# Forty-six products split a second time instead of thirty-six, in a 4096 x 4096 x 4096 product with GELU

## The chip, the cores and the metric

The kernel runs on one NeuronCore of one Trainium2 chip. The metric is the device time of one execution in microseconds, lower being better; "time" below is the median of several runs, and the profiled execution has its own time beside its span.

## The reference

```python
def reference(a, b):            # a, b: 4096 x 4096 float32
    x = np.matmul(a, b)
    return 0.5 * x * (1 + np.tanh(np.sqrt(2 / np.pi) * (x + 0.044715 * x**3)))
```

The output is 4096 x 4096 float32. The kernel loads A and B as 16-bit floats; checks on the sizes of the inputs, made on the way, choose at the end whether the result stands or a slower general path runs (it does not here).

## The kernel before

**Two levels of seven products.** A and B are cut in halves each way, and the four quadrants of the output come from seven products instead of eight (Winograd's form): P1 = A11 B11, P2 = A12 B21, P3 = S4 B22, P4 = A22 T4, P5 = S1 T1, P6 = S2 T2, P7 = S3 T3, with block sums S1 = A21 + A22, S2 = S1 - A11, S3 = A11 - A21, S4 = A12 - S2, and T1 to T4 likewise of B. In the code S1 lies in the cells SA, S3 in ST, and S2 in SB, where S4 later overwrites it.

The output is made in 16 *groups*: four row blocks (512 rows in each half) by four column blocks (512 columns in each half). In a group each of the seven is a product of 512 x 2048 by 2048 x 512, cut in four *quarters* along the middle (512 each).

An **unsplit** product (`quarters`) is 4 quarters x 4 row tiles x 4 matmuls of 128 x 128 by 128 x 512: 64 matmuls (L535). A **split** one (`split`, `stage`, `part_pe`) applies the same scheme once more inside the product: seven parts of 2 row tiles x 8 matmuls of 128 x 128 by 128 x 256, 112 matmuls (L911), the first of each row of P1's part being 512 wide when it also clears the bank. It asks for four sums of A's inner blocks (`inner_sum`, called 5, 6, 3 and 7 by their parts, L841), for sums of B's inner blocks, and for additions inside the PSUM banks (`copy_part` on ACT, L924; `add_part` on DVE, L928). Two products run in turn, stage by stage, one in bank set X and one in Y (`both`, `run`).

**Where B's operands of a split product come from** is its mode in the table GROUPS: `f` fetches seven pieces from HBM that an earlier group stored; `m` fetches the four quarters and makes the pieces on chip with four sums on DVE (`made_split`); `ms` does that and stores the pieces for later (`made_stored`); `um` leaves the product unsplit but makes and stores the pieces; no entry is unsplit. Every such fetch or store moves 512 KB.

**Order of work.** Groups 0 to 6 read B raw and store T1 to T4 as *units* (`raw_group`); those in RAW_CUT split P3 with `made_here` beside the quarters of P4. Groups 7 to 15 (`late_group`) fetch units. While groups 7 and 11 (TURNS) run, the next row block of A is loaded and turned (`turn_quad`); one quadrant of it is turned ahead, in group 10 (EARLY). Each engine's order is written out by a planner (`Plan`): every operation gets a cost from COST, a due time worked back from PE's order, and a place; PE's order is that of the program text. Fetches go out on POOL's queue, stores on SP's (`dma`, L759).

SBUF holds 28 *cells* of 512 KB: 16 for B, 4 each for SB, SA and ST. A split product takes cells for its quarters or pieces of B and for its sums of A; a cell is handed on in order of time, so a fetch into it waits for PE or DVE to have read what was there. Results leave the banks through `add_bank` (DVE, L1124) and `copy_out` (ACT, L1118), then GELU on ACT (L1102, L1112), then the store.

In the code, `combine2` (L841) is every block or inner sum, and `products` (L535) the unsplit matmuls. The groups' numbers are 0-based; group 12 is the first of the last row block.

Of the kernel before, what the change touches and what calls it, by code (L numbers as in the profile page):

```python
# [75 lines left out]
    "POOL": 0.56, "SP": 0.4,  # L76
}

def modes_of(tail=None, **kw):
    got = {name: mode for mode, names in kw.items() for name in names.split()}
    return got if tail is None else {**got, "tail": tail}
# [15 lines left out]
EARLY = {10: 3}  # L100
TURNS = {7: 2, 11: 3}


class Op:
    __slots__ = ("n", "eng", "dur", "fn", "deps", "succ", "key", "left", "ready", "start", "end", "size", "weight")


class Plan:
# [3 lines left out]

    def add(self, eng, dur, fn, r=(), w=(), size=0, batch=None, after=(), slack=18.0, weight=1.0):
        o = Op()
        o.weight = weight
# [24 lines left out]
        return o  # L140
# [37 lines left out]
    def schedule(self):  # L178
# [23 lines left out]
        while n_done < len(self.ops):  # L202
# [31 lines left out]
            o.start = at  # L234
            free[best] = at + o.dur
            n_done += 1
# [55 lines left out]
def half_path(  # L292
# [455 lines left out]
    def dve(cost, fn, r, w, **kw):  # L748
        return plan.add("DVE", COST[cost], fn, r=r, w=w, **kw)

    def act(cost, fn, r, w, **kw):
        return plan.add("ACT", COST[cost], fn, r=r, w=w, **kw)

# [8 lines left out]
    def c(x):  # L762
        return ("c", x)
# [19 lines left out]

    UNIT, PIECE = {}, {}

    def unit(nb, name):
        if (nb, name) not in UNIT:
            t = f"u{nb}{name}"
            UNIT[nb, name] = dram_pool.tile([P, QPH, CELL], F16, name="k_unit", tag=t)
        return UNIT[nb, name]  # L790

    def piece(nb, name, p):
# [55 lines left out]

    def inner_sum(op, x, y):
        t = new_cell()  # L850
        combine2(cell(t).rearrange("p (jj m) -> p jj m", jj=NJ // 2), [c(t)], x, y, op)
        return t
# [35 lines left out]

    def split(s, a_src, b, bits):
        z = Split()  # L890
        z.s, z.a, z.bits, z.sum = s, a_src, bits, {}
        z.b, z.prepare = b
        return z
# [5 lines left out]
    def part_pe(z, p):  # L899
# [19 lines left out]
        if p in z.sum and p != "6":  # L919
            free_cells.append(z.sum.pop(p))  # L920

    def copy_part(dst, src, cost="part"):
        (d, dt), (x, xt) = dst, src
        act(cost, lambda: nc.scalar.copy(out=d, in_=x), [xt] if xt else [], [dt])  # L924
# [5 lines left out]
    def stage(z, k):  # L930
# [8 lines left out]

        if k == 1:  # L940
            z.sum["5"] = inner_sum(1, a_inner(z.a, "21"), a_inner(z.a, "22"))
            z.sum["6"] = inner_sum(-1, as_inner(z.sum["5"]), a_inner(z.a, "11"))
            for r in range(2):
                copy_part(of("12", r), (zeros[:, 0:1].to_broadcast([P, HC]), None), "zero")
            part_pe(z, "5")
            z.j5 = new_small()
            for r in range(2):
                copy_part(j(z.j5, r), of("12", r))
            part_pe(z, "1")
            for r in range(2):  # L950
                copy_part(of("11", r), of("21", r))
        elif k == 2:
            part_pe(z, "2")
            part_pe(z, "6")
            z.sum["3"] = inner_sum(-1, a_inner(z.a, "12"), as_inner(z.sum["6"]))
            free_cells.append(z.sum.pop("6"))
            j2 = new_small()
            for r in range(2):
                copy_part(j(j2, r), of("21", r))
            for r in range(2):  # L960
                add_part(of("12", r), of("12", r), j(j2, r))
            free_small.append(j2)
        elif k == 3:
            z.sum["7"] = inner_sum(-1, a_inner(z.a, "11"), a_inner(z.a, "21"))
# [454 lines left out]

    sets = {"X": 0}  # L1420

    def late_group(gi, modes, turn=None):

# [4 lines left out]
        cut = {name for name in NAMES if modes.get(name, "u") in ("f", "m", "ms")}  # L1428
        tail_v = "P7" in cut or "P3" in cut and modes.get("tail") == "v"
# [6 lines left out]
        if gi in EARLY or turn:  # L1436
            k = new_unit()
            pairs = (k[0], k[2])
        if gi in EARLY:
            turn_quad(EARLY[gi], "11", slots["a"]["21"], pairs)  # L1440
            free_cells.extend(k)
        source = {
            "P1": raw("11"), "P2": raw("12"), "P5": blk(SA), "P6": blk(SB), "P7": blk(s3), "P3": blk(SB), "P4": raw("22")
        }

        def work(name, s, fresh, done=None, bits=False):
# [4 lines left out]
            b = {"f": fetched, "m": made_split, "ms": made_stored}[mode](nb, name)  # L1451
            return stages_of(split(s, source[name], b, bits), done)

# [39 lines left out]

        x4 = {}
        if turn:
            def p4_done(i, s=X):
                x4[i] = copy_out(s, i)

            run(work("P4", X, True, p4_done))
            turn_quad(turn, "22", slots["a"]["22"], pairs)  # L1500
            if gi - 1 not in EARLY:
                turn_quad(turn, "11", slots["a"]["21"], pairs)
            X, Y = Y, X
        both(("P1", X, True, p1_done, "P6" not in cut), ("P2", Y, not alone, p2_done))
        if last:
            final_answer()
        if turn:
            turn_quad(turn, "12", slots["a"]["11"], pairs)
        both(("P6", X, False, p6_done, not tail_v), ("P5", Y, True, p5_done, not tail_v))
        if last:  # L1510
            final_read()
        block(SB, -1, raw("12"), blk(SB))
        if turn:
            turn_quad(turn, "21", slots["a"]["12"], pairs)

# [5 lines left out]
        def c22_v(i):  # L1521
# [7 lines left out]
            else:  # L1529
                y[i] = new_small()  # L1530
                add_bank(v[i], X, i, y[i])
            out_of(gi, i, 1, 1, y[i])

# [5 lines left out]
        def c21(i):  # L1539
# [5 lines left out]
            else:  # L1545
                r0, c0 = place(gi, i, 1, 0)
                for k, (queue, eng) in enumerate((("SP", nc.sync), ("ACT", nc.scalar))):
# [6 lines left out]
                        r=[("f", f)], size=0.35)  # L1554

        def c21_turn(i):
            f = x4[i]
# [7 lines left out]
        if tail_v:  # L1565
            both(("P7", X, True, c22_v, True), ("P3", Y, True, c12))
            if turn:
                for i in range(RT):
                    c21_turn(i)
            else:  # L1570
                run(work("P4", X, False, c21))
            sets["X"] = Y
        else:
# [5 lines left out]
            elif "P3" in cut:  # L1579
                for i in range(RT):  # L1580
                    add_bank(u[i], Y, i)
                run(work("P4", X, False, c21), work("P3", Y, True, c12))
            else:
                run(work("P4", X, False, c21))
                run(work("P3", Y, False, c12))
            sets["X"] = X
        if turn:
# [53 lines left out]
    with tc.manual_schedule():  # L1641
# [18 lines left out]
        for slot in ("11", "12", "21", "22"):  # L1660
            free_cells.extend(slot_cells(slots["b"][slot]))
        for gi, modes in GROUPS.items():
            if gi == LAST:
                final_checks()
            late_group(gi, modes, TURNS.get(gi))
        plan.emit()
# [37 lines left out]
```

## Time and profile before

| | |
|---|---|
| median of 3 runs | 1529.7 us (1527.08 to 1529.83) |
| profiled execution | 1530.25 us, span 1528.7 us |
| PE matmuls in the profile | 8974, busy 1515.7 us |
| of these 512 columns, unsplit (L535) in the two largest groups | 2176 + 2176 |
| DVE, ACT, POOL busy | 1053.6, 653.9, 460.9 us |
| HBM | 320.34 MB read, 144.71 MB written |
| mean granted TensorE clock | 0.999 |

In a row of a group, the line of the kernel, the engine and the operation come first, then what is written and read by name, sizes and count; after the bar the busy time and the mean of one in ns; after the second bar the idle time just before them and what ended it. A row of the order of time has its start, its length, and in brackets the idle time before it. Matmuls are pipelined, so the length of one alone (380 ns) is not its pace.

### The profile page before, as it was taken

The numbers are of one execution on the slowest core, as the hardware profiler recorded it, in microseconds if no ns is written. First come the engines' busy times: TensorE is split into PE (matmuls) and PEld (weight loads), VectorE is DVE, ScalarE is ACT, GpSimd is POOL, SyncE is SP. The second block draws the span as 40 slices with busy tenths as digits, with TensorE's granted clock in tenths as the row PEclk, the third lists the DMA queues.
The fourth block names the chain that finished last, engine by engine and source line by source line (L and its number), as shares of the span: only waits on it lengthen the run. The fifth ranks groups of instructions, "written<-read, shape, count | busy, mean of one in ns | idle before, by whom it ended". The sixth has DMA issues, their size and how long they took to land.

```text
span 1528.7 us, 23988 instructions
## 1 busy us (share of the span) xinstructions
PE 1515.7 (99%) x8974; PEld 878.8 (57%) x8974; DVE 1053.6 (69%) x1236; ACT 653.9 (43%) x1483; POOL 460.9 (30%) x831
## 2 busy tenths in 40 slices
PE   9999999999999999999999999999999999999998
PEld 4444454544445545455446666556456858887684
DVE  2596868847678598794377655664468987977682
ACT  5445244464954545446742221523453323231332
POOL 7765341442205334123411112213220213223130
PEclk9999999999999999999999999999999999999999
DMA  9999599999949999979987878979995667878593
GB/s 175 196 208 220 98 284 322 243 255 303 251 171 229 284 289 279 338 180 265 280 267 273 294 243 279 303 272 281 270 247 196 244 220 249 296 255 306 199 316 136
DMA packets 199467, 382.84 MB, mean 250 GB/s; under 512 B 20144, under 2 KB 110512, under 8 KB 199344
## 3 DMA queue, kind: packets, MB, share of 16 engines
q0 software_dynamic: 140592, 236.51, 65.2%
q1 hardware_dynamic: 58608, 144.60, 24.9%
q8 instruction: 72, 1.18, 0.3%
q14 instruction: 51, 0.42, 0.1%
q10 hardware_dynamic: 144, 0.13, 0.0%
HBM read 320.34 MB, written 144.71 MB: 304 GB/s over the span
## 4 chain that ended last, share of the span: by engine, by line
PE 89%; DMA 6%; DVE 2%; POOL 1%; issue 1%; ACT 1%; ACTq 0%; POOLq 0%; DVEq 0%
PE acc L535 59%; PE acc L911 27%; PE acc L570 2%; DMA stage<-in_a_dram 2%; DMA bR<-in_a_dram 2%; DMA bR<-in_b_dram 2%; DMA bR<-k_unit 1%; POOL stage L437 1%; DVE y L549 1%; DVE aD L520 1%; POOL bR L437 0%; DVE aT L412 0%; ACT y L1158 0%; DVE aD L549 0%; POOL bR L759 0%
## 5 line engine op out<-in xcount | busy, mean ns | idle before, releaser
L535 PE MATMUL acc<-bR,aT 128*128 128x512 f16 x2176 | 478.7, 380 | 2.4 <-DMA bR<-k_unit 2.4
L535 PE MATMUL acc<-bR,aD 128*128 128x512 f16 x2176 | 478.4, 379 | 0.8 <-ACT y L1112 0.8
L535 PEld LDWEIGHTS <-aD 128*128 128x128 f16 x2272 | 222.4, 98 | 264.6 <-issue 4.9
L535 PEld LDWEIGHTS <-aT 128*128 128x128 f16 x2240 | 219.6, 98 | 261.7 <-issue 4.9
L759 POOL DMA_DIRECT2D bR<-k_unit x255 | 145.6, 573 | 560.5 <-PE acc L535 270.3
L841 DVE TENSOR_TENSOR bR<-bR 128x2048 f16<-128x2048 f16 x181 | 218.0, 1221 | 84.7 <-DMA bR<-in_b_dram 38.1
L911 PE MATMUL acc<-bR 128*128 128x256 f16 x1984 | 232.4, 273 | 0.0
L759 POOL DMA_DIRECT2D bR<-in_b_dram x288 | 155.4, 544 | 250.2 <-PE acc L535 154.0
L911 PEld LDWEIGHTS <-bR 128*128 128x128 f16 x1984 | 194.1, 98 | 30.6 <-DVE bR L841 0.3
L1124 DVE TENSOR_TENSOR y<-acc,y 128x512 f32<-128x512 f32 x240 | 154.9, 686 | 41.7 <-PE acc L911 23.0
L1192 ACT ACTIVATE y<-bR 128x1024 bf16<-128x1024 f16 x128 | 129.6, 1051 | 108.4 <-DVE y L1197 91.0
L924 ACT COPY y<-acc 128x256 f32<-128x256 f32 x144 | 53.5, 371 | 205.3 <-PE acc L911 205.2
L1102 ACT ACTIVATE y<-y 128x512 f32<-128x512 f32 x180 | 107.6, 627 | 70.6 <-DVE y L1124 69.5
L1118 ACT COPY y<-acc 128x512 f32<-128x512 f32 x116 | 66.5, 585 | 157.2 <-PE acc L535 108.9
L911 PE MATMUL acc<-bR,aD 128*128 128x256 f16 (+1 forms) x864 | 103.8, 274 | 0.0
L928 DVE TENSOR_TENSOR acc<-acc,y 128x256 f32<-128x256 f32 x144 | 59.7, 429 | 59.7 <-ACT y L924 37.1
L1158 ACT ACTIVATE y<-bR 128x512 f16<-128x512 f16 x128 | 80.5, 629 | 38.1 <-DMA bR<-in_a_dram 29.2
L841 DVE TENSOR_TENSOR aD<-aT,aD 128x2048 f16<-128x2048 f16 x60 | 72.9, 1220 | 32.3 <-PE acc L535 32.3
L841 DVE TENSOR_TENSOR aD<-aD,aT 128x2048 f16<-128x2048 f16 x60 | 72.5, 1220 | 29.0 <-PE acc L535 29.0
L911 PEld LDWEIGHTS <-aD 128*128 128x128 f16 x864 | 84.5, 98 | 13.0
L1197 DVE TENSOR_TENSOR y<-y 128x1024 bf16<-128x1024 bf16 x120 | 82.6, 688 | 13.2 <-ACT y L1192 9.6
L412 DVE STREAM_TRANSPOSE aT<-stage 128x1024 uint32<-128x1024 uint32 (+1 forms) x27 | 35.7, 1349 | 63.3 <-DMA stage<-in_a_dram 53.8
(86 smaller groups left out, 1273.8 us busy)
## 6 DMA issues: line engine op xcount, KB each, us to landing
bR<-k_unit POOLq DMA_DIRECT2D x255, 512.0 KB, 6.8
out_dram<-y SPq DMA_DIRECT2D x251, 256.0 KB, 6.5
k_unit<-bR SPq DMA_DIRECT2D x112, 512.0 KB, 6.5
bR<-in_b_dram POOLq DMA_DIRECT2D x384, 128.0 KB, 6.7
k_piece<-bR SPq DMA_DIRECT2D x36, 512.0 KB, 5.5
bR<-k_piece POOLq DMA_DIRECT2D x36, 512.0 KB, 5.8
bR<-in_a_dram POOLq DMA_DIRECT2D x64, 256.0 KB, 8.4
stage<-in_a_dram POOLq DMA_DIRECT2D x48, 256.0 KB, 7.7
```

The source lines that it names most:

```text
L535: nc.tensor.matmul(acc, sa[:, j // 2, i * P : (i + 1) * P, j % 2], sb[:, j, :], start=start and j == 0, stop=stop and j == 3, skip_group_c ...
L759: return plan.add(queue, COST[queue], lambda: eng.dma_start(out=dst, in_=src), r=r, w=w, size=MOVE[what], weight=weight, **kw)
L841: nc.vector.tensor_tensor(out=dst, in0=xa, in1=ya, op=ALU.add if op > 0 else ALU.subtract)
L911: nc.tensor.matmul(PS[s][i][:, :] if wide else PS[s][i][:, w * HC : (w + 1) * HC], sa[:, j // 2, r * P : (r + 1) * P, j % 2], rhs(j, wide) ...
L924: act(cost, lambda: nc.scalar.copy(out=d, in_=x), [xt] if xt else [], [dt])
L928: dve("part", lambda: nc.vector.tensor_tensor(out=d, in0=xa, in1=ya, op=ALU.add), [xt, yt], [dt])
L1102: act("gelu", lambda: nc.scalar.activation(t, t, ACT.Gelu_apprx_tanh), [("f", f)], [("f", f)])
L1118: act("copy", lambda: nc.scalar.copy(out=sm(f), in_=bank(s, i)), [], [("f", f), ("p", s, i)])
L1124: dve("add", lambda: nc.vector.tensor_tensor(out=sm(g), in0=bank(s, i), in1=sm(f), op=ALU.add), [("f", f)], [("f", g), ("p", s, i)])
L1158: act("weigh", lambda x=x, r=r, s=s, f=f: nc.scalar.activation(small[f].bitcast(F16)[:, : 2 * RUN], s[:, x, :], ACT.Square, accum_out=t[:, ...
L1192: act("square", lambda t=t, src=src: nc.scalar.activation(t, src, ACT.Square), [c(cx)], [("f", f)], slack=60.0)
L1197: dve("add16", lambda t=t, u=u: nc.vector.tensor_tensor(out=u, in0=u, in1=t, op=ALU.add), [("f", f)], [("f", e)], slack=60.0)
```

## The change

- Which products are split changes throughout: raw groups 1 and 2 split nothing (RAW_CUT), groups 7 to 15 split 43 products instead of 31, mostly in mode `m`; raw groups 5 and 6 store pieces of P7, and of P6 and P3.
- S1, S2, S3 are made once in a row block and kept; S4 is written into A21's cells, which no product reads after S1 and S3 exist. Groups that turn A keep the old way.
- In groups 8, 9, 13 and 14 P4 is split too. There P3 no longer shares its bank set's content with P4, and in groups 8 and 13 P4 is left over and run at the start of the next group beside P1 (`pending`), which then takes an order of its own.
- Inside a split product sum 6 overwrites sum 5's cell and sum 3 overwrites sum 6's (IN_PLACE). A's inner sums of P1 and P3 are stored in group 12, those of P3 fetched in group 14 (`a_sum`).
- The early turn of group 10 moves from the group's start to its end.
- The planner keeps an engine for EVERY's shorter time per operation (start to start), while the result still counts as ready after COST's time.

```diff
+EVERY = {
+    "sum": 1.145, "sum/2": 0.62, "add": 0.61, "add16": 0.62, "copy": 0.49, "gelu": 0.54, "square": 0.97, "weigh": 0.65,
+    "part": 0.345, "turn": 1.2,
+}
...
-RAW_MAKES = {}
-RAW_CUT = (1, 2, 4, 5, 6)
+IN_PLACE = 3
+RAW_MAKES = {5: ("P7",), 6: ("P6", "P3")}
+RAW_CUT = (4, 5, 6)
 GROUPS = {
-    7: {},
-    8: modes_of(ms="P2 P5 P7"),
-    9: modes_of(ms="P2 P5 P7"),
-    10: modes_of(ms="P2 P5 P7"),
-    11: modes_of(m="P5"),
-    12: modes_of(m="P2 P5 P7 P1 P6"),
-    13: modes_of(f="P2 P5 P7", m="P1 P6 P3"),
-    14: modes_of(f="P2 P5 P7", m="P1 P6"),
-    15: modes_of(f="P2 P5 P7", m="P1 P6"),
+    7: modes_of(m="P1 P6", tail="v"),
+    8: modes_of(m="P4 P5 P6", ms="P7", um="P1", tail="v"),
+    9: modes_of(m="P2 P3 P4 P7", ms="P1 P6"),
+    10: modes_of(m="P1 P2 P5 P6 P7", tail="v", early="end"),
+    11: modes_of(m="P2 P5"),
+    12: modes_of(f="P3 P6", m="P1 P2 P7", store="P1 P3"),
+    13: modes_of(f="P7", m="P1 P2 P5 P6", ms="P3 P4", tail="v"),
+    14: modes_of(f="P6", m="P1 P2 P3 P4 P5 P7", fetch="P3", tail="v"),
+    15: modes_of(f="P7", m="P2 P3 P5 P6"),
 }
-EARLY = {10: 3}
 TURNS = {7: 2, 11: 3}
...
             o.start = at
-            free[best] = at + o.dur
+            free[best] = at + o.every
...
+    def a_sum(z, p, op, x, y, t=None):
+        if z.kept is None:
+            return inner_sum(op, x, y, t)
+        how, *key = z.kept
+        if how == "fetch":
+            t = new_cell() if t is None else t
+            dma("POOL", cell(t), a_piece(*key, p)[:, :], [("as", *key, p)], [c(t)], "unit")
+            return t
+        t = inner_sum(op, x, y, t)
+        dma("SP", a_piece(*key, p)[:, :], cell(t), [c(t)], [("as", *key, p)], "unit")
+        return t
...
+            x5 = z.sum["5"]
             part_pe(z, "5")
+            if IN_PLACE & 1:
+                free_cells.remove(x5)
+                z.sum["6"] = a_sum(z, "6", -1, as_inner(x5), a_inner(z.a, "11"), x5)
...
-            z.sum["3"] = inner_sum(-1, a_inner(z.a, "12"), as_inner(z.sum["6"]))
-            free_cells.append(z.sum.pop("6"))
+            x6 = z.sum.pop("6")
+            z.sum["3"] = a_sum(z, "3", -1, a_inner(z.a, "12"), as_inner(x6), x6 if IN_PLACE & 2 else None)
...
-        block(SB, -1, blk(SA), raw("11"))
+        if new_mb or not held_sums:
+            block(SB, -1, blk(SA), raw("11"))
...
+        if s4_in_slot:
+            if new_mb:
+                s4 = raw("21")
+                for q in range(QPH):
+                    dst, toks = a_quarter(s4, q)
+                    combine2(dst, toks, a_quarter(raw("12"), q), a_quarter(blk(SB), q), -1)
+            held_sums.append(gi)
...
+        if pending:
+            run(pending(), work("P1", X, True, p1_done_f, "P6" not in cut))
...
+            both(("P2", Y, True, p2_done_f), ("P6", X, False, p6_done_f))
...
+            both(("P5", Y, True, p5_done_f), ("P7", X, True, lambda i: c22_v(i), "P4" not in cut))
+            both(("P3", Y, True, lambda i: c12(i), not last), ("P4", X, "P4" in cut, lambda i: c21(i), not last))
+            if modes.get("early") == "end":
+                early()
...
+            elif "P4" in cut:
+                sets["X"] = Y
+                return lambda: work("P4", X, True, c21, True)
```

More of the change, by code (lines that the diff above doesn't have):

```diff
@@ L77, with modes_of @@
 }
-def modes_of(tail=None, **kw):
-    got = {name: mode for mode, names in kw.items() for name in names.split()}
-    return got if tail is None else {**got, "tail": tail}
-RAW_MAKES = {}
-RAW_CUT = (1, 2, 4, 5, 6)
-GROUPS = {
-    7: {},
-    8: modes_of(ms="P2 P5 P7"),
-    9: modes_of(ms="P2 P5 P7"),
-    10: modes_of(ms="P2 P5 P7"),
-    11: modes_of(m="P5"),
-    12: modes_of(m="P2 P5 P7 P1 P6"),
-    13: modes_of(f="P2 P5 P7", m="P1 P6 P3"),
-    14: modes_of(f="P2 P5 P7", m="P1 P6"),
-    15: modes_of(f="P2 P5 P7", m="P1 P6"),
+EVERY = {
+    "sum": 1.145, "sum/2": 0.62, "add": 0.61, "add16": 0.62, "copy": 0.49, "gelu": 0.54, "square": 0.97, "weigh": 0.65,
+    "part": 0.345, "turn": 1.2,
+}
+def modes_of(tail=None, early=None, store="", fetch="", **kw):
+    got = {name: mode for mode, names in kw.items() for name in names.split()}
+    got["kept"] = {**{n: "store" for n in store.split()}, **{n: "fetch" for n in fetch.split()}}
+    return {**got, **{k: v for k, v in (("tail", tail), ("early", early)) if v}}
+IN_PLACE = 3
+RAW_MAKES = {5: ("P7",), 6: ("P6", "P3")}
+RAW_CUT = (4, 5, 6)
+GROUPS = {
+    7: modes_of(m="P1 P6", tail="v"),
[7 more added lines that the diff above has]
+    15: modes_of(f="P7", m="P2 P3 P5 P6"),
 }
-EARLY = {10: 3}
 TURNS = {7: 2, 11: 3}
 class Op:
-    __slots__ = ("n", "eng", "dur", "fn", "deps", "succ", "key", "left", "ready", "start", "end", "size", "weight")
+    __slots__ = ("n", "eng", "dur", "fn", "deps", "succ", "key", "left", "ready", "start", "end", "size", "weight", "every")
 class Plan:
@@ L111, in __init__, with add @@
         self.ops, self.state, self.now = [], {}, BUSY["PE"]
-    def add(self, eng, dur, fn, r=(), w=(), size=0, batch=None, after=(), slack=18.0, weight=1.0):
+    def add(self, eng, dur, fn, r=(), w=(), size=0, batch=None, after=(), slack=18.0, weight=1.0, every=None):
         o = Op()
+        o.every = dur if every is None else every
         o.weight = weight
@@ L748, in dve @@
     def dve(cost, fn, r, w, **kw):
-        return plan.add("DVE", COST[cost], fn, r=r, w=w, **kw)
+        return plan.add("DVE", COST[cost], fn, r=r, w=w, every=EVERY.get(cost), **kw)
     def act(cost, fn, r, w, **kw):
-        return plan.add("ACT", COST[cost], fn, r=r, w=w, **kw)
+        return plan.add("ACT", COST[cost], fn, r=r, w=w, every=EVERY.get(cost), **kw)
     def dma(queue, dst, src, r, w, what, **kw):
@@ L790, in unit, with a_piece @@
         return UNIT[nb, name]
+    def a_piece(mb, name, p):
+        if (mb, name, p) not in A_PIECE:
+            t = f"a{mb}{name}{p}"
+            A_PIECE[mb, name, p] = dram_pool.tile([P, CELL], F16, name="k_asum", tag=t)
+        return A_PIECE[mb, name, p]
     def piece(nb, name, p):
@@ L887, in half_path, with split @@
         pass
-    def split(s, a_src, b, bits):
+    def split(s, a_src, b, bits, kept=None):
         z = Split()
-        z.s, z.a, z.bits, z.sum = s, a_src, bits, {}
+        z.s, z.a, z.bits, z.sum, z.kept = s, a_src, bits, {}, kept
         z.b, z.prepare = b
@@ L963, in stage @@
         elif k == 3:
[L964 removed]
+            z.sum["7"] = a_sum(z, "7", -1, a_inner(z.a, "11"), a_inner(z.a, "21"))
             part_pe(z, "7")
@@ L1418, in raw_group, with late_group @@
             slots["a"] = {"11": old["21"], "12": old["11"], "21": old["12"], "22": old["22"]}
-    sets = {"X": 0}
-    def late_group(gi, modes, turn=None):
+    sets, held_sums = {"X": 0}, []
+    def late_group(gi, modes, turn=None, pending=None):
         mb, nb = groups[gi]
@@ L1435, in late_group, with early, fourth @@
             block(ST, -1, raw("11"), raw("21"))
-        if gi in EARLY or turn:
+        def early():
+            k = new_unit()
+            turn_quad(groups[gi][0] + 1, "11", slots["a"]["21"], (k[0], k[2]))
+            free_cells.extend(k)
+        held_sums.clear()
+        s4_in_slot = not turn and modes.get("early") != "start"
+        if modes.get("early") == "start":
+            early()
[6 more added lines that the diff above has]
+            held_sums.append(gi)
+        if turn:
             k = new_unit()
             pairs = (k[0], k[2])
-        if gi in EARLY:
-            turn_quad(EARLY[gi], "11", slots["a"]["21"], pairs)
-            free_cells.extend(k)
+        def fourth():
+            if not s4_in_slot:
+                block(SB, -1, raw("12"), blk(SB))
         source = {
-            "P1": raw("11"), "P2": raw("12"), "P5": blk(SA), "P6": blk(SB), "P7": blk(s3), "P3": blk(SB), "P4": raw("22")
+            "P1": raw("11"), "P2": raw("12"), "P5": blk(SA), "P6": blk(SB), "P7": blk(s3), "P3": raw("21") if s4_in_slot else blk(SB), "P4": raw("22")
         }
@@ L1451, in work @@
             b = {"f": fetched, "m": made_split, "ms": made_stored}[mode](nb, name)
-            return stages_of(split(s, source[name], b, bits), done)
+            how = modes.get("kept", {}).get(name)
+            return stages_of(split(s, source[name], b, bits, how and (how, mb, name)), done)
         p1, u, v, y = {}, {}, {}, {}
@@ L1492, in both, with p2_done_f, p6_done_f, p1_done_f @@
                 run(work(*xs), work(*ys))
[L1494 to L1514, printed above, removed]
+        def p2_done_f(i):
+            f = new_small()
+            add_bank(p1[i], Y, i, f)
+            out_of(gi, i, 0, 0, f)
+        def p6_done_f(i):
+            if "P6" in cut:
+                u[i] = add_bank(p1[i], X, i)
+            else:
+                free_small.append(p1[i])
+                u[i] = copy_out(X, i)
+        def p1_done_f(i):
+            p1[i] = copy_out(X, i)
+        def p5_done_f(i):
+            v[i] = new_small()
+            add_bank(u[i], Y, i, v[i])
         def c12(i):
@@ L1554, in c21, with p4_done @@
                         r=[("f", f)], size=0.35)
+        if pending:
+            run(pending(), work("P1", X, True, p1_done_f, "P6" not in cut))
+            if last:
+                final_answer()
+            both(("P2", Y, True, p2_done_f), ("P6", X, False, p6_done_f))
+            if last:
+                final_read()
+            fourth()
+            both(("P5", Y, True, p5_done_f), ("P7", X, True, lambda i: c22_v(i), "P4" not in cut))
+            both(("P3", Y, True, lambda i: c12(i), not last), ("P4", X, "P4" in cut, lambda i: c21(i), not last))
+            if modes.get("early") == "end":
+                early()
+            sets["X"] = Y
+            return None
+        x4 = {}
+        if turn:
+            def p4_done(i, s=X):
+                x4[i] = copy_out(s, i)
+            run(work("P4", X, True, p4_done))
+            turn_quad(turn, "22", slots["a"]["22"], pairs)
+            if "early" not in GROUPS.get(gi - 1, ()):
+                turn_quad(turn, "11", slots["a"]["21"], pairs)
+            X, Y = Y, X
+        both(("P1", X, True, p1_done, "P6" not in cut), ("P2", Y, not alone, p2_done))
+        if last:
+            final_answer()
+        if turn:
+            turn_quad(turn, "12", slots["a"]["11"], pairs)
+        both(("P6", X, False, p6_done, not tail_v), ("P5", Y, True, p5_done, not tail_v))
+        if last:
+            final_read()
+        fourth()
+        if turn:
+            turn_quad(turn, "21", slots["a"]["12"], pairs)
         def c21_turn(i):
@@ L1566, in late_group @@
             both(("P7", X, True, c22_v, True), ("P3", Y, True, c12))
+            if modes.get("early") == "end":
+                early()
             if turn:
@@ L1582, in late_group @@
                 run(work("P4", X, False, c21), work("P3", Y, True, c12))
+                if modes.get("early") == "end":
+                    early()
             else:
@@ L1585, in late_group @@
                 run(work("P3", Y, False, c12))
+                if modes.get("early") == "end":
+                    early()
             sets["X"] = X
```

21 lines of the change are left out of this document (14 added, 7 removed).

## The prediction

> **What bounds the kernel now.** I read the page's busy times first, then who PE waited for, then PE's own order of time, then DVE and the DMA landings in the stretches that the change fills.
>
> ```profile
> PE 1515.7 (99%) x8974; PEld 878.8 (57%) x8974; DVE 1053.6 (69%) x1236; ACT 653.9 (43%) x1483; POOL 460.9 (30%) x831
> PE acc L535 <- DMA bR<-k_unit: 2.4, 1, 2.4
> PE acc L535 <- DVE aD L520: 1.8, 1, 1.8
> PE acc L544 <- DVE table L717: 1.5, 1, 1.5
> PE acc L535 <- DVE y L549: 1.0, 2, 0.9
> ```
>
> PE works 99% of the span. The list of its waits (microseconds in total, times, longest) says the same from the other side: four of them pass 1 us, three of those belong to the first group and the start, and only one, 2.4 us for a fetched unit, lies in the groups that the change touches. So the time is the columns that PE streams, plus that one wait. A busy PE could still be a slow one, so I take its pace from starts, not from the modelled durations:
>
> ```profile
> 1059.79 55.42 PE L535 MATMUL acc<-bR,aT 128*128 128x512 f16 x256
> 1115.05 3.62 PE L535 MATMUL acc<-bR,aD 128*128 128x512 f16 x16
> ...
> 1270.33 7.15 PE L911 MATMUL acc<-bR 128*128 128x256 f16 x64
> 1277.32 1.91 PE L911 MATMUL acc<-bR,aT 128*128 128x256 f16 x16
> ```
>
> From 1059.79 to 1115.05 there are 256 matmuls of 512 columns: 0.2159 us each. From 1270.33 to 1277.32 there are 64 of 256 columns: 0.1092 us each, just over half. An unsplit product is 64 of the first, 13.81 us; a split one is 112 of the second, 12.23 us.
>
> **The one wait, and its real price.**
>
> ```profile
> 994.57 1.91 PE L911 MATMUL acc<-bR 128*128 128x256 f16 x16
> 998.87 5.30 PE L535 MATMUL acc<-bR,aT 128*128 128x512 f16 x16 [2.39 <-DMA bR<-k_unit]
> 1004.00 1.25 PE L911 MATMUL acc<-bR 128*128 128x256 f16 x10
> ...
> 998.90:1004.00 5.10, 5.10 (x16) 1.96 (x16) 3.58 (x3) 1.76 (x3) 0.00 (x0) 0.67 0.40 162
> ...
> 112.20 2.82 PE L535 MATMUL acc<-aD 128*128 128x512 f16 x12 [0.85 <-DVE y L549]
> 115.20 1.02 PE L535 MATMUL acc<-aD 128*128 128x512 f16 x4 [0.18 <-DVE y L549]
> 118.08 1.24 PE L535 MATMUL acc<-aD 128*128 128x512 f16 x5 [1.85 <-DVE aD L520]
> ```
>
> The 16 matmuls after the 2.39 us gap last from 998.87 to 1004.00, 5.13 us where 16 x 0.2159 = 3.45 are due: the granted clock in that row of the stretches is 0.67. The wait therefore cost 2.39 + 1.68 = 4.1 us. A gap of 1.85 us at 118.08 has no such tail (1.24 us for 5). So a stall costs its own length up to about 2 us, and 1.7 more from about 2.4. [...]
>
> **The change, part by part.** Counts come from the order of the two built programs.
>
> *PE.* 640 matmuls of 512 columns go (ten products, 64 each) and 1120 split ones come; of the split ones six more than before have 512 columns (the first matmul of P1's part where the bank is cleared). Net: 634 x 0.2159 = 136.9 us out, 1114 x 0.1092 = 121.6 us in: **-15.2 us**. All of it lies on the path, since PE has no other slack. Raw groups 1 and 2 lose their split product, which is in these counts.
>
> *The old wait.*
>
> ```profile
> 954.64 24.22 DMA bR<-in_a_dram x2
> 985.55 13.27 DMA bR<-k_unit
> ```
>
> These two pieces of the chain that ended last come just before it. In group 10 the early turn of the next block's A stood at the group's start, so eight 256 KB loads ran on POOL's queue ahead of the fetches for P1 and P2, and a unit then took 13.27 us. The turn now stands at the end of the group, beside P3 and unsplit P4, where DVE and PE want no new fetch at once. I take the 4.1 us as gone; if another fetch is late there it stays. Bounds: 0 to **-4.1**.
>
> *DVE.* Kept block sums remove 44 sums (S2 and S4 in the second to fourth group of a block, eight each but four in group 11). A split product adds four sums of A and four additions inside the banks; an operand made on chip adds four sums of B. Net over the program: 51 more sums and 8 half ones, 40 more bank parts, 28 more whole-bank additions.
>
> ```profile
> L841 DVE TENSOR_TENSOR bR<-bR 128x2048 f16<-128x2048 f16 x181 | 218.0, 1221 | 84.7 <-DMA bR<-in_b_dram 38.1 <-PE acc L911 16.1 <-DMA bR<-k_unit 13.9
> L1124 DVE TENSOR_TENSOR y<-acc,y 128x512 f32<-128x512 f32 x240 | 154.9, 686 | 41.7 <-PE acc L911 23.0 <-PE acc L535 15.9 <-ACT y L1118 1.4
> L928 DVE TENSOR_TENSOR acc<-acc,y 128x256 f32<-128x256 f32 x144 | 59.7, 429 | 59.7 <-ACT y L924 37.1 <-PE acc L911 21.3
> ...
> 1209.51 1.09 DVE L928 TENSOR_TENSOR acc<-acc,y 128x256 f32<-128x256 f32 x3 [0.44 <-PE acc L911]
> ...
> 1212.90 1.22 DVE L841 TENSOR_TENSOR bR<-bR 128x2048 f16<-128x2048 f16 x1
> 1214.03 1.22 DVE L841 TENSOR_TENSOR bR<-stage 128x2048 f16<-128x2048 f16 x1
> 1215.17 1.88 DVE L1124 TENSOR_TENSOR y<-acc,y 128x512 f32<-128x512 f32 x3
> ...
> 1218.10 2.48 DVE L1124 TENSOR_TENSOR y<-acc,y 128x512 f32<-128x512 f32 x4
> ```
>
> In full durations (1.22, 0.686, 0.429; half sum half of it) that is 51 x 1.22 + 8 x 0.61 + 40 x 0.429 + 28 x 0.686 = 104 us, so DVE 1158 us of some 1512, 77%: never the bound as a whole. What counts is where it sits. Back to back, a sum takes 1.14 us from start to start (1212.90 to 1214.03), a whole-bank addition (2.48 - 0.69)/3 = 0.60, a part (1.09 - 0.43)/2 = 0.33. Now the densest stretches, with A22's products put where they run:
> - Groups 13 and 14 (13 split products and one P4 that slides from 13 into 14, nothing unsplit): PE 196 half-row steps of 8 x 0.1092 = 0.874, with eight wide starts, 172.1 us. DVE 100 sums, 56 parts, 56 additions: 114 + 18.5 + 33.6 = 166.1 us, 97% of PE.
> - Groups 8 and 9: PE 64 x 0.863 + 140 x 0.874 + 0.9 = 178.5; DVE 96 sums, 8 half sums, 40 parts, 52 additions: 109.4 + 4.6 + 13.2 + 31.2 = 158.4, 89%.
> - Groups 5 and 6 gain 4 and 8 sums for P7, P3 and P6's stored pieces, 4.6 and 9.1 us, in groups of 95 us (96 x 0.863 + 14 x 0.874); they had unsplit products to hide in.
>
> ```profile
> 1193.60:1218.00 24.40, 24.40 (x224) 21.88 (x225) 23.79 (x30) 6.97 (x18) 4.73 (x9) 1.00 0.54 186
> 1331.70:1345.50 13.80, 13.80 (x67) 6.23 (x65) 13.54 (x16) 2.91 (x6) 2.36 (x3) 1.00 0.84 321
> ```
>
> In these rows (length, then busy PE, PEld, DVE, ACT, POOL, clock, DMA) DVE is busy 23.79 of 24.40 us and 13.54 of 13.80 while PE never stops: 97% can be held, but shown for 25 us, not for 172. Every small wait of DVE for a bank (0.44 us in the row above) has no spare place in groups 13 and 14. Bounds: 0, if the order fills all of them; 172 x 3% = 5 us, if DVE loses another 3% beyond the 97. I take 2.
>
> *A's sums in place.* P6's sum now overwrites P5's cell, and P3's overwrites P6's. That puts a wait on DVE: the sum for part 6 may start only when PE has read part 5. Behind it in DVE's fixed order stand the next product's sums and the bank parts; PE's part 6 waits for it. Between part 5 and part 6 PE has eight half-row steps (or four and an unsplit quarter, 3.5 us either way), 7.0 us, for one sum of 1.22: covered. Where A's sums are fetched instead of made (P3 of group 14 alone), the same hand-over goes through POOL: behind that fetch stand the 16 unit fetches of group 15.
>
> ```profile
> bR<-k_unit POOLq DMA_DIRECT2D x255, 512.0 KB, 6.8
> ...
> bR<-k_unit POOLq DMA_DIRECT2D x50, 512.0 KB, 8.3
> ...
> bR<-k_piece POOLq DMA_DIRECT2D x12, 512.0 KB, 5.5
> ```
>
> The columns end with median microseconds to landing: over the whole run, in the stretch 900 to 1060 us, and for pieces in group 14 of this kernel. From part 6 read to part 3 needed PE has eight steps, 7.0 us. A 512 KB fetch lands in 5.5 to 8.3: between 0 and 1.5 us late, 0.5 taken.
>
> *DMA.* POOL's fetches of 512 KB go from 291 to 283, SP's stores from 148 to 156: nothing in sum. Group 12 rises from 28 to 42 of them (eight are A's kept sums), with 16 outputs of 256 KB: 26.2 MB in the group's 89 us (32 x 0.863 + 70 x 0.874), 294 GB/s. Groups 8 to 10 of before have 40 and as many outputs, 25.2 MB in 92 us, 274 GB/s, and had one late fetch in three groups. Bounds 0 to 4.1; I take 1.5.
>
> *ACT.* 40 copies out, 20 zero fills and 20 bank copies, under 0.4 us each, on an engine at 43%: hidden; without that cover each is 0.4 us.
>
> **Sum.** The profiled execution took 1530.25 us (span 1528.7). 1530.25 - 15.2 - 4.1 = 1510.9, the floor; + 2 + 0.5 + 1.5 = 1514.9. The three runs have their median 0.55 lower, at 1529.7; I give 1515.
>
> **Rivals.**
> - *DVE becomes the bound* in groups 13 and 14. If the back-to-back overlap is lost because most operations wait singly for PE or ACT, DVE needs 100 x 1.22 + 56 x 0.429 + 56 x 0.686 = 184.4 us against PE's 172.1: 12.3 more, 1510.9 + 12.3 = 1523. For it: single waits of 0.44 us are common where parts are added. Against: overlap holds in the rows above, in a stretch of split products only. [...]
> - *Fetches land late* at the hand-over from one made pair to the next: the next pair's four B quarters may be fetched only into cells that the present pair frees after its parts 7 and 4. One late fetch of 2.4 us costs 4.1. It decides from the fifth: 1510.9 + 5 x 4.1 = 1531, slower than before. With about 18 hand-overs in groups 9 to 15, every second one late gives 1510.9 + 9 x 4.1 = 1548. For it: 8.3 us landings. Against: group 12 of before had the same pattern, four made products in a row, without one wait of PE.
> - *The smaller matmuls don't keep their pace* once nothing else lies between, because the weight load is what sets 0.109. PEld is busy 21.88 of 24.40 us in such a stretch, so it is not. If it were 3% slower, 1114 x 0.1092 x 3% = 3.6 us: 1518.5.
>
> **How the numbers follow.** Forecast, with its sums from 1510.5 to 1518: 0.68. DVE as the bound, up to 1524: 0.14. One to four late fetches, 1518 to 1527: 0.10. Five or more: 0.06. Slow small matmuls: 0.02. The range from 1509.5 (0.5 below the floor with its 0.55, rounded) to 1525 leaves out the last fetch cases. A difference under 0.2%, 3 us, cannot be told from none; so faster is below 1526.6 (0.90), the same 0.04, slower 0.06.
>
> **What would show it.** Right: PE's busy time near 1500, no row of its waits above 2 us in groups 7 to 15, the granted clock 1.00 in every stretch, DVE 95% or more in groups 13 and 14. Wrong: a wait of L923 (split matmuls) for DVE sums adding to 10 us (first rival), for DMA into bR several times with clock below 0.8 after it (second), or a start-to-start pace of split matmuls above 0.111.

## Result and the profile after

The changed kernel takes 1512.45 us (1510.38 to 1512.8) where the kernel before takes 1529.76: the ratio of the two is 0.9877 (95% interval 0.9843 to 0.9911). In a later job on another chip (run e10, the changed kernel once more) it was 1512.67 beside 1528.3, ratio 0.9904 (0.9888 to 0.9920). So it is faster by 1.0 to 1.2%, 16 to 17 us by the medians; 1515 was forecast. The profiled execution took 1512.8 us, its span 1511.2.

The page's busy times and its landings, changed kernel:

```profile
PE 1499.0 (99%) x9454; PEld 924.7 (61%) x9454; DVE 1148.4 (76%) x1372; ACT 672.7 (45%) x1555; POOL 451.9 (30%) x823
bR<-k_unit POOLq DMA_DIRECT2D x259, 512.0 KB, 7.8
```

PE issues 480 matmuls more and is busy 16.7 us less. DVE has gained 95 us and PE is still at 99%. Whom PE waited for, all its rows (microseconds in total, times, longest):

```profile
PE acc L541 <- DVE aD L526: 1.9, 1, 1.9
PE acc L550 <- DVE table L723: 1.5, 1, 1.5
PE acc L541 <- DVE y L555: 1.2, 2, 1.1
PE acc L541 <- ACT y L559: 1.0, 2, 0.6
PE acc L576 <- ACT y L559: 0.7, 1, 0.7
PE acc L923 <- DVE bR L853: 0.5, 2, 0.3
PE acc L923 <- DMA bR<-k_asum: 0.3, 1, 0.3
PE acc L923 <- DVE y L1155: 0.2, 1, 0.2
```

The first five belong to the start and to the first group. Only the last three lie in work that the change touches, 1.0 us in all, and the 2.4 us for a fetched unit is gone; in e10's profile the waits in groups 7 to 15 are down to one of 0.27 us. PE in order of time shows where the last three lines fall, all but 0.16 us of them in group 14:

```profile
678.79 2.12 PE L923 MATMUL acc<-bR,aD 128*128 128x512 f16 x16 [0.16 <-DVE bR L853]
1321.39 2.04 PE L923 MATMUL acc<-bR 128*128 128x256 f16 x16 [0.32 <-DVE bR L853]
1397.21 3.87 PE L923 MATMUL acc<-bR,aT 128*128 128x512 f16 x32 [0.21 <-DVE y L1155]
1401.34 1.92 PE L923 MATMUL acc<-bR 128*128 128x256 f16 x16 [0.26 <-DMA bR<-k_asum]
```

The stretches (columns as in the prediction) from the start of group 13 to the end of group 14, whole and two of its pieces:

```profile
1243.80:1417.20 173.40, 172.60 (x1569) 153.15 (x1568) 161.32 (x207) 61.35 (x152) 38.18 (x69) 1.00 0.76 263
1268.00:1293.00 25.00, 25.00 (x232) 22.40 (x230) 24.99 (x33) 7.63 (x20) 5.42 (x9) 1.00 0.63 205
1363.00:1388.00 25.00, 25.00 (x232) 22.40 (x230) 25.00 (x31) 8.11 (x21) 4.73 (x9) 1.00 0.62 209
```

In 173.4 us PE stops for 0.8. DVE is busy 93% over the whole and without a gap in the two pieces of 25 us; it keeps up, just. The pace of the split matmuls is that of the kernel before: 64 of them take 6.99 us from start to start here, 0.1092 us each.

```profile
1255.85 7.15 PE L923 MATMUL acc<-bR 128*128 128x256 f16 x64
1262.84 1.91 PE L923 MATMUL acc<-bR,aT 128*128 128x256 f16 x16
```

### The profile page after: what moved, and what is told of

It is laid out like the page before. It is cut to its first block, busy times and chain, and to the rows that moved or that the text cites. A ratio compares the mean times of both kernels' runs of the same rounds, so it can differ in the third digit from the quotient of the medians.

```text
span 1511.2 us, 25214 instructions
## 1 busy us (share of the span) xinstructions
PE 1499.0 (99%) x9454; PEld 924.7 (61%) x9454; DVE 1148.4 (76%) x1372; ACT 672.7 (45%) x1555; POOL 451.9 (30%) x823
## 5 line engine op out<-in xcount | busy, mean ns | idle before, releaser
L541 PE MATMUL acc<-bR,aT 128*128 128x512 f16 x1920 | 421.6, 379 | 0.0
L541 PE MATMUL acc<-bR,aD 128*128 128x512 f16 x1792 | 391.5, 379 | 0.0
L853 DVE TENSOR_TENSOR bR<-bR 128x2048 f16<-128x2048 f16 (+1 forms) x251 | 297.6, 1202 | 99.1 <-DMA bR<-k_unit 29.4
L541 PEld LDWEIGHTS <-aT 128*128 128x128 f16 x1984 | 194.0, 98 | 227.1
L541 PEld LDWEIGHTS <-aD 128*128 128x128 f16 x1888 | 184.5, 98 | 224.9 <-issue 4.6
L923 PE MATMUL acc<-bR 128*128 128x256 f16 x2752 | 320.4, 273 | 0.6 <-DVE bR L853 0.3
L923 PEld LDWEIGHTS <-bR 128*128 128x128 f16 x2752 | 269.0, 98 | 38.6 <-DVE bR L853 0.6
L948 ACT COPY y<-acc 128x256 f32<-128x256 f32 x184 | 68.2, 371 | 181.6 <-PE acc L923 174.8
L923 PE MATMUL acc<-bR,aT 128*128 128x256 f16 x1056 | 126.2, 274 | 0.2 <-DVE y L1155 0.2
L923 PEld LDWEIGHTS <-aT 128*128 128x128 f16 x1056 | 103.3, 98 | 14.3 <-issue 0.4
L853 DVE TENSOR_TENSOR aD<-aT 128x2048 f16<-128x2048 f16 x60 | 71.9, 1219 | 46.0 <-PE acc L541 45.3
L923 PEld LDWEIGHTS <-aD 128*128 128x128 f16 x816 | 79.8, 98 | 11.9 <-issue 0.4
```

Source lines behind the costliest of these rows:

```text
L541: nc.tensor.matmul(acc, sa[:, j // 2, i * P : (i + 1) * P, j % 2], sb[:, j, :], start=start and j == 0, stop=stop and j == 3, skip_group_c ...
L853: nc.vector.tensor_tensor(out=dst, in0=xa, in1=ya, op=ALU.add if op > 0 else ALU.subtract)
L923: nc.tensor.matmul(PS[s][i][:, :] if wide else PS[s][i][:, w * HC : (w + 1) * HC], sa[:, j // 2, r * P : (r + 1) * P, j % 2], rhs(j, wide) ...
```

## Experiments

Each is one edit of the changed kernel, or of the kernel before where it says so. Times are medians beside the kernel before on the same chip, whose medians were 1528.66 (e1 to e4), 1529.06 (e5 to e8) and 1528.3 (e9 to e12).

**e1: the early turn's place alone, in the kernel before.**

```diff
-        if gi in EARLY:
-            turn_quad(EARLY[gi], "11", slots["a"]["21"], pairs)
...
             both(("P7", X, True, c22_v, True), ("P3", Y, True, c12))
+            if gi in EARLY:
+                k = new_unit()
+                turn_quad(EARLY[gi], "11", slots["a"]["21"], (k[0], k[2]))
...
```

> The kernel before with one edit: group 10's early turn of the next block's A stands after P7 and P3 instead of at the group's start. Theory (the turn's eight loads held up the fetches of P1 and P2, and that one wait of 2.39 us cost 4.1 with the slow clock behind it): the wait of PE for a fetched unit is gone, clock 1.00 throughout, 1529.7 - 4.1 = 1525.6 us. Rival (the stores of pieces in groups 8 to 10 load the queues, the turn's place is indifferent): the wait stays, 1529 to 1530.

1527.55 us, ratio 1.0003 (0.9985 to 1.0022). In its profile the wait for a fetched unit is gone, so the mechanism holds; the 4.1 us do not show. The two medians differ by 1.1 us, and the interval includes no difference at all.

**e9: the kernel before once more.**

> The kernel before, unchanged, profiled once more. Theory A (the late fetch in group 10 belongs to the kernel): PE waits for a fetched unit near 999 us again, about 2.4 us with a slow clock behind it. Theory B (it was that execution's luck, DMA landings vary): no such wait, span 1525 to 1526.

PE in order of time:

```profile
998.15 3.61 PE L535 MATMUL acc<-bR,aT 128*128 128x512 f16 x16 [1.35 <-DMA bR<-k_unit]
```

The wait is there again, at the same place, but 1.35 us long, and the 16 matmuls behind it take 3.61 us instead of 5.30, at a granted clock of 1.00 from 990 to 1000 us: no slow clock. It belongs to the kernel; its price was one execution's.

**e2: the block sums not kept.**

```diff
-        s4_in_slot = not turn and modes.get("early") != "start"
+        s4_in_slot = False
```

> The changed kernel, with S2 and S4 made anew in every group, in SB: 44 more sums on DVE, nothing else changed. In groups 13 and 14 DVE's work rises by 16 sums to 166.1 + 18.2 = 184.3 us against PE's 172.1. Theory A (DVE stands just under PE there, so the kept sums are what lets the splitting pay): 5 to 12 us of PE waiting for DVE in groups 12 to 15, up to 3 in group 9; 1518 to 1526. Theory B (DVE has room, the kept sums are worth nothing): 1512 to 1514.

1533.44 us, ratio 1.0034 (1.0018 to 1.0050): all of the gain is gone and some more. Its waits of PE for DVE, apart from those of the first group:

```profile
PE acc L923 <- DVE acc L952: 7.7, 4, 3.0
PE acc L923 <- DVE bR L853: 6.9, 8, 1.7
PE acc L923 <- DVE y L1155: 1.7, 1, 1.7
PE acc L541 <- DVE y L1155: 0.8, 1, 0.8
```

They sum to 17.1 us, 0.16 of it before group 7. Each of the 14 stops costs some 0.16 us more than its row says: the wait is counted from the end of the matmul before (0.273 us long), where in an unbroken run the next would have started 0.109 after its start. Before the two longest waits, which end at 1345.83 and 1400.18, DVE did not stop (length, then busy PE, PEld, DVE, ACT, POOL, clock, DMA):

```profile
1340.00:1345.80 5.80, 3.14 (x29) 2.67 (x28) 5.80 (x7) 0.00 (x0) 1.98 (x4) 1.00 0.82 252
1394.00:1400.10 6.10, 3.17 (x30) 2.69 (x28) 6.10 (x9) 0.00 (x0) 1.57 (x3) 1.00 0.88 273
```

So PE waits because DVE has too much to do: theory A, and more than its 12 us of waits, since DVE is late not only in groups 13 and 14 but, by the times of the waits, in 10, 11 and 15 too. With 46 products split, 44 sums of 1.14 us decide between 16 to 17 us gained and 5 lost.

**e3: A22's product left whole in the four groups.**

```diff
-    8: modes_of(m="P4 P5 P6", ms="P7", um="P1", tail="v"),
+    8: modes_of(m="P5 P6", ms="P7", um="P1", tail="v"),
```

and P4 likewise out of groups 9, 13 and 14.

> The changed kernel with P4 unsplit in groups 8, 9, 13 and 14 (42 products split), so nothing slides into the next group. Theory (columns decide): four times 13.81 - 12.23 = 1.58 us more, less 0.9 for eight wide starts that go: 5.5 more, 1518. Rival (the last four cost DVE what they save PE): 1512 to 1514, with fewer waits for DVE.

1518.97 us, ratio 0.9937 (0.9921 to 0.9954), 6.3 to 6.5 us above the changed kernel's medians, which are from other chips. Columns decide: 5.5 were worked out, and no wait of the late groups passes 0.8 us.

**e6: the planner's old view of DVE's and ACT's occupation.**

```diff
-EVERY = {
-    "sum": 1.145, "sum/2": 0.62, "add": 0.61, "add16": 0.62, "copy": 0.49, "gelu": 0.54, "square": 0.97, "weigh": 0.65,
-    "part": 0.345, "turn": 1.2,
-}
+EVERY = {}
```

> The changed kernel, where the planner again takes COST's time for an engine's occupation as well (EVERY empty); the same work, another order on DVE and ACT. Theory A (the order only has to be near right, DVE does what comes): 1512 to 1514. Theory B (with DVE at 97% of PE in groups 13 and 14, an order planned on 1.19 a sum instead of 1.145 makes PE wait in the wrong places): 2 to 6 us of waits of PE for DVE more, 1514 to 1519.

1518.78 us, ratio 0.9932 (0.9917 to 0.9948), 6 us above the changed kernel with the same operations on every engine. Its waits of PE in the late groups:

```profile
PE acc L920 <- DVE bR L850: 2.3, 2, 1.7
PE acc L920 <- ACT acc L945: 1.4, 3, 0.6
PE acc L920 <- DVE acc L949: 1.4, 2, 1.0
```

5.1 us, 3.7 of it for DVE, where the changed kernel has 1.0. So an order planned on the longer times brings some 4 us of waits; the rest of the 6 is not shown to come from the order. In the profiled execution (1519.17 us) 1.7 us were lost elsewhere, in the first group, behind a wait that the changed kernel has as well; the first row of each pair is e6, the second the changed kernel:

```profile
119.61 5.30 PE L538 MATMUL acc<-aD 128*128 128x512 f16 x16 [1.85 <-DVE aD L523]
120.03 3.61 PE L541 MATMUL acc<-aD 128*128 128x512 f16 x16 [1.85 <-DVE aD L526]
...
119.60:124.90 5.30, 5.29 (x17) 2.09 (x17) 2.64 (x4) 1.98 (x4) 4.23 (x8) 0.68 1.14 247
120.03:123.48 3.45, 3.45 (x17) 1.56 (x17) 2.59 (x4) 1.89 (x3) 3.00 (x6) 1.00 1.12 258
```

The same 16 matmuls behind the same wait of 1.85 us ran at a granted clock of 0.68 here and of 1.00 there. All fourteen profiles have this wait; in thirteen the matmuls behind it kept their pace of 0.216 us, only in e6 were they slow.

**e7: A's inner sums neither stored nor fetched.**

```diff
-    12: modes_of(f="P3 P6", m="P1 P2 P7", store="P1 P3"),
+    12: modes_of(f="P3 P6", m="P1 P2 P7"),
...
-    14: modes_of(f="P6", m="P1 P2 P3 P4 P5 P7", fetch="P3", tail="v"),
+    14: modes_of(f="P6", m="P1 P2 P3 P4 P5 P7", tail="v"),
```

> The changed kernel without stored sums of A: group 12 stores none, and P3 of group 14 makes its four on DVE, 4.6 us more of DVE where it is at 97%, for 12 transfers of 512 KB less. Theory A (DVE is full there): 1 to 4 us more of waits for DVE, 1513 to 1517; the 0.3 us wait for a fetched sum is gone. Theory B (the transfers cost as much as they save): 1512 to 1513.

1514.99 us (1511.68 to 1516.49), ratio 0.9912 (0.9897 to 0.9927). Its interval overlaps the changed kernel's two: not settled. The profile (of the 1511.68 run) has one wait of 0.94 us for DVE in group 14, where the changed kernel has 0.32 and 0.21 for DVE and 0.26 for the fetched sum.

**e12: A's sums in cells of their own.**

```diff
-IN_PLACE = 3
+IN_PLACE = 0
```

> The changed kernel with A's sums 6 and 3 in cells of their own instead of over sums 5 and 6. DVE and PE do the same work; a split product holds up to one cell more, so fetches of the next pair start later. Theory A (cells are what the in-place sums buy, and the hand-over of cells is nearly full): one to three waits for fetched units, 1514 to 1522. Theory B (cells are not short; the in-place sums only add a wait to DVE): 1511 to 1513.

1522.74 us, ratio 0.9962 (0.9952 to 0.9972): 10 us of the gain go, in a kernel that computes the same with the same number of operations. Its waits (the profiled run took 1519.27):

```profile
PE acc L923 <- DVE bR L853: 3.0, 5, 1.0
PE acc L923 <- DVE y L1155: 2.4, 2, 1.6
PE acc L923 <- DMA bR<-k_unit: 2.1, 2, 1.6
```

Theory A, in part: two fetches come late for PE, and in seven places PE waits for DVE (one of them, 0.16 us, the changed kernel has too). In three of the seven, which end at 900.06, 972.44 and 1375.18, DVE itself had just waited for a fetched unit:

```profile
898.78 1.22 DVE L853 TENSOR_TENSOR bR<-bR 128x2048 f16<-128x2048 f16 x1 [0.49 <-DMA bR<-k_unit]
971.16 2.36 DVE L853 TENSOR_TENSOR bR<-bR 128x2048 f16<-128x2048 f16 x2 [0.31 <-DMA bR<-k_unit]
1368.97 1.22 DVE L853 TENSOR_TENSOR bR<-bR 128x2048 f16<-128x2048 f16 x1 [1.92 <-DMA bR<-k_unit]
```

Before the other three DVE was busy without such a wait; the edit also changes DVE's order. So writing sum 6 over sum 5 is not a detail: it is worth 10 us, part of it by leaving cells for the next pair's quarters to be fetched in time. How the 10 us divide between cells and order is not shown.

**e4, e11: 49 products, by P3 of raw groups 1 and 2 and P1 of group 15.**

```diff
-RAW_CUT = (4, 5, 6)
+RAW_CUT = (1, 2, 4, 5, 6)
...
-    15: modes_of(f="P7", m="P2 P3 P5 P6"),
+    15: modes_of(f="P7", m="P1 P2 P3 P5 P6"),
```

> The changed kernel with three more products split, 49 in all: P3 in raw groups 1 and 2 as before the change, and P1 of group 15. Theory (columns decide as long as DVE stays under PE; groups 1, 2 and 15 are at 70 to 80%): 3 x 1.58 - 0.4 = 4.3 us less, 1508. Rival (each further split product brings a late fetch or a wait for DVE of its own): 1511 to 1514.

> 49 products split (P3 of raw groups 1 and 2 and P1 of group 15 more), beside the changed kernel. By columns 4.3 us less; by the first look, where PE waited 1.7 us after group 2 and about 1 us more in groups 14 and 15, 1 us less. Theory A (the waits belong to the splits): 0.5 to 1.5 us less than the changed kernel, not to be told from none. Theory B (they were one execution's): 3 to 4 us less.

1511.41 us, ratio 0.9896 (0.9880 to 0.9913), then 1513.12, 0.9894 (0.9878 to 0.9909), beside 0.9904 for the changed kernel on the second chip. The 4.3 us of columns are not there. PE in order of time in e4 shows where some of them went:

```profile
341.73 1.02 PE L541 MATMUL acc<-bR,aD 128*128 128x512 f16 x4 [0.84 <-ACT y L1143]
343.16 1.02 PE L541 MATMUL acc<-bR,aD 128*128 128x512 f16 x4 [0.41 <-ACT y L1143]
344.59 5.77 PE L541 MATMUL acc<-bR,aD 128*128 128x512 f16 x26 [0.41 <-ACT y L1143]
```

In group 3, PE waits 1.7 us for ACT to read a bank; the kernel before has 0.8 of it at this place and the changed kernel, which splits nothing in groups 1 and 2, none. In groups 14 and 15 three waits for DVE add 1.1. In e11's profile (of a run of 1516.45 us) these waits are there again, with 1.6 us more for ACT in groups 3 and 4 and 2.0 for DVE in groups 7 and 11. Not to be told from the changed kernel.

**e8: 49 products, by three late ones.**

```diff
-    10: modes_of(m="P1 P2 P5 P6 P7", tail="v", early="end"),
+    10: modes_of(m="P1 P2 P3 P5 P6 P7", tail="v", early="end"),
...
-    12: modes_of(f="P3 P6", m="P1 P2 P7", store="P1 P3"),
+    12: modes_of(f="P3 P6", m="P1 P2 P5 P7", store="P1 P3"),
...
-    15: modes_of(f="P7", m="P2 P3 P5 P6"),
+    15: modes_of(f="P7", m="P1 P2 P3 P5 P6"),
```

> The changed kernel with three more products split in late groups, 49 in all: P3 of group 10, P5 of group 12, P1 of group 15, all made on chip. Theory (columns decide; these groups have DVE at 70 to 85%): 3 x 1.37 = 4.1 us less, 1508.3. Rival (group 12 and 15 no longer give groups 13 and 14 room before and after, so DVE's backlog shows): 1 to 4 us of waits for DVE, 1509.5 to 1512.5.

1526.38 us, ratio 0.9984 (0.9975 to 0.9993): fewer columns for three more products, and 14 us more in time. Both theories missed. PE, and then POOL's queue, in order of time:

```profile
1045.36 7.07 PE L541 MATMUL acc<-bR,aT 128*128 128x512 f16 x32
1060.09 5.28 PE L541 MATMUL acc<-bR,aT 128*128 128x512 f16 x12 [7.66 <-DMA bR<-k_unit]
...
1021.15 2.34 POOL L765 DMA_DIRECT2D bR<-in_a_dram  x4 [6.31 <-PE acc L923]
1035.88 0.57 POOL L765 DMA_DIRECT2D bR<-k_unit  x1 [12.39 <-PE acc L923]
1037.09 0.55 POOL L765 DMA_DIRECT2D bR<-k_unit  x1 [0.64 <-PE acc L923]
1037.62 1.77 POOL L765 DMA_DIRECT2D bR<-in_a_dram  x3
```

With P3 split beside P7, group 10 holds two products' quarters and sums to its end. POOL stands 12.39 us waiting for PE to free a cell; then the fetches for P4 and the turn's loads go out together, and PE waits 7.66 us for a unit, with the 12 matmuls behind it at half pace (5.28 us, 2.6 due). (The wait lies in group 10, where P3 is the one product that the edit adds; that P3 is its cause is argued, not tried alone.) Another 5.5 us are waits for DVE from group 12 on. The room that the changed table leaves in these groups was in use.

**e5: the price of a wait.**

```diff
...
+                if i == 2:
+                    for n in GAPS.get(at_gap["gi"], {}).get(at_gap["n"], ()):
+                        dve("sum", lambda n=n: nc.vector.tensor_tensor(
+                            out=cell(x)[:, :n], in0=cell(x)[:, :n], in1=cell(x)[:, :n], op=ALU.max), [], [c(x)])
                 quarter_pe(s, i, a_op, x, fresh and q == 0)
```

> The changed kernel, with twelve forced waits of PE in unsplit quarters of groups 7 and 11: between the second and the third row tile of a quarter, DVE rewrites part of the B cell with itself, in one to three operations of 256 to 2048 columns. The waits should last from about 1.0 to 3.8 us, 27 in sum. Theory A (the prediction's price: from about 2.4 us the clock is slow behind the wait and 1.7 us are lost besides): five of the twelve are followed by matmuls at a granted clock near 0.67; 1512.5 + 27 + 8.5 = 1548. [...] Theory C (it hangs on where the wait falls): waits of like length have both outcomes.

1561.18 us. PE's rows behind seven of the twelve forced waits, which stand in brackets, shortest first; eight matmuls at full pace last 1.89, 48 last 10.5:

```profile
734.51 1.89 PE L541 MATMUL acc<-bR,aT 128*128 128x512 f16 x8 [1.78 <-DVE bR L891]
1097.60 5.34 PE L541 MATMUL acc<-bR,aT 128*128 128x512 f16 x24 [1.91 <-DVE bR L891]
1165.03 12.22 PE L541 MATMUL acc<-bR,stage 128*128 128x512 f16 x48 [2.05 <-DVE bR L891]
1117.41 2.87 PE L541 MATMUL acc<-bR,aT 128*128 128x512 f16 x8 [2.31 <-DVE bR L891]
779.91 12.22 PE L541 MATMUL acc<-bR,stage 128*128 128x512 f16 x48 [2.58 <-ACT y L1200]
1142.07 3.55 PE L541 MATMUL acc<-bR,aD 128*128 128x512 f16 x8 [3.51 <-DVE bR L891]
796.44 2.76 PE L541 MATMUL acc<-bR,stage 128*128 128x512 f16 x8 [4.31 <-DVE bR L891]
```

In this run no wait up to 1.91 us was followed by a slow stretch; the seven from 2.05 us on all were, and each lost 1.5 to 2.6 us to the end of its stretch, some 12 in sum. The granted clock was 0.50 to 0.87 in the windows with those seven stretches, 1.00 in the ones behind the waits of 1.65 and 1.91 us. But two waits of e2 were longer and were not:

```profile
1345.83 1.91 PE L923 MATMUL acc<-bR,aT 128*128 128x256 f16 x16 [2.68 <-DVE acc L952]
1400.18 1.91 PE L923 MATMUL acc<-bR,aD 128*128 128x256 f16 x16 [3.01 <-DVE acc L952]
```

Their granted clock stayed at 1.00. Theory C across the kernels, and without a floor at 2 us: in e6 one wait of 1.85 us was followed by a slow stretch, in e2 one of 3.01 was not. The wait of 1.85 us had both outcomes at one place in the same work, so neither its length nor the work around it decides alone. What does, these runs do not tell. The prediction's threshold of about 2.4 us does not hold as a rule: waits of 1.85 (e6), 2.05 and 2.31 us were followed by a slow stretch too.

## Why the prediction was right, point by point

- **Columns, -15.2 us.** Right. PE's busy time fell by 16.7 us, and 1.7 of that is the slow stretch behind the old wait, which leaves 15.0. e3 prices four of the ten products at 6.3 to 6.5 us where 5.5 were worked out. The split matmuls kept their pace of 0.1092 us, so the rival of slow small matmuls falls.
- **The old wait, -4.1 us.** The mechanism was right (e1 removes the wait by moving the turn alone), its size was not: e9 shows 1.35 us without a slow clock, and over the runs e1 gains 1.1 us, not to be told from none. The step that failed is the one that took one execution's price for the kernel's. Its rule that a stall up to about 2 us costs only itself rested on the wait of 1.85 us at 118.08; in e6 that same wait cost 1.7 us more.
- **DVE, +2 us.** 0.7 us measured (0.16, 0.32 and 0.21). That DVE stands just under PE in groups 13 and 14 was right: 166 us of work were counted, and it was busy 161 of 173 there. That is 93%, under the 95 that the prediction named as a sign: 66.12 of 73.60 us before 1317.40, in group 13, and 95.20 of 99.80 after it. How near the edge was, e2 shows: 44 sums bring 17.1 us of waits; the rival "DVE becomes the bound" is what the kernel is without the kept sums, or, by 3.7 us of waits for DVE, without the planner's shorter times (e6).
- **The fetched sum, +0.5 us.** It was the tightest step named, and the only DMA that PE waited for in groups 7 to 15: 0.26 us, and 0.27 in the second profile. The chain that ended last begins with it, 7.71 us of transfer from 1393.59 on.
- **DMA, +1.5 us.** Nothing: PE waited for no unit in groups 7 to 15, though the median landing rose from 6.8 to 7.8 us.
- **Sum.** Floor 1510.9 for the profiled execution, plus 0.95 of the four late waits, plus 0.8 for the other waits behind the start, is 1512.6; it took 1512.8. The 0.8 are 1.6 more in the first group (4.8 us against 3.2, work that the change does not touch) less 0.8 in group 3 that went with the splits of groups 1 and 2.
- **What was luck.** The medians before, less 15.2, are 1513.1 to 1514.6, so only 0.4 to 2.1 us are left for the old wait less the new ones. The forecast put 4.1 for the one and 4.0 for the others. Both were some 3 us too large, and they cancel; that 1515 is so near owes something to that.
- **In place sums.** The prediction called their wait covered, which is right, and gave them no worth, which is wrong: e12 prices them at 10 us, in part through the cells.
- **Late fetches.** The rival did not come in the changed kernel, but e8 and e12 show that it stands three products or one cell a product away.

## What to carry to other kernels

When PE is the bound at 99%, count its columns first: the gain is theirs, and the rest of the change has to be judged by whether it keeps every other engine from being late. Count the second engine's work by stretches, by starts and not by durations, and look at what frees the buffers: here 44 sums were worth all of the gain, the cell that a product saves by writing its sums in place 10 us of it, and the planner's taking 1.145 us for a sum instead of 1.19 (and the like for others) 4 to 6. One profiled wait has a place that repeats and a size that does not (2.39 us, then 1.35 in e9), and the slow stretch behind it was there in the first profile and not in the second; price both from several executions.

## What the runs showed of the hardware

- DVE was busy 24.99 and 25.00 of 25 us, while PE did not stop (the changed kernel, from 1268 and from 1363); in the kernel before, back-to-back sums start 1.13 us apart though each lasts 1.22 (1212.90 and 1214.03 in the prediction's rows).
- In these runs the length of a wait of PE did not say whether the clock was lower behind it. Behind one of 1.85 us in the first group the matmuls kept their pace in thirteen profiles (3.61 us for 16, at a granted clock of 1.00, in the changed kernel) and not in one (e6: 5.30 us for 16, at 0.68); behind one of 3.01 us the clock was 1.00 (e2).
- In these profiles a stop of PE costs some 0.16 us more than the wait shown, since the modelled end of the matmul before lies that much behind the start that the next would have had (0.273 us long, 0.109 apart); for the fourteen waits in e2, 17.1 us in sum, that makes over 2 us more, an estimate from 14 x 0.16.
